# Hybrid block on one core: output projection with 512 moving tokens, its norm spread over later tiles, retention products in place, second buffer for B

## Chip, cores and metric

One Trainium2 chip, one of its cores, one launch. The metric is the device time of that core in microseconds (us); the time before is the median of three runs.

## What is computed

A block for 1024 tokens of 1024 channels, all in float32: a mixer with a retention branch and an S5 branch (a state-space scan) side by side, a projection with residual, attention to a memory of 256 tokens, another projection with residual, and a last norm. Cut to its steps:

```
h = rms_norm(x, norm1_g);  proj = h @ w_in            # 1024 -> q, k, v, g_ret, u, g_s5
ret = retention(rotary(q), rotary(k), v, ret_gn_g) * silu(g_ret)
ssm = s5_branch(u, s5 parameters, glu) * silu(g_s5)
x = x + concat([ret, ssm]) @ w_out
h2 = rms_norm(x, norm2_g);  m = rms_norm(mem, norm_mem_g)
s = einsum(h2 @ wq, m @ wk) * 256 ** -0.5             # 4 heads of 256
o = softmax(s) @ (m @ wv)
x = x + o @ wo
return rms_norm(x, norm_f_g)        # y = x * rsqrt(mean(x * x) + eps) * norm_f_g
```

## The kernel before

**Layout and products.** Activations stand turned: channels on the 128 partitions, tokens along the row. Each large product is made of three matmuls (`mm3`, lines 100 to 103): both operands are split into a high part, rounded to the type float32r, and the low part that is left, and high times high, high times low and low times high are summed in PSUM. `proj_t` (line 105) holds 128x128 weights stationary and moves 512 tokens past them; `proj_nat` (line 511, for `v`) and, before the change, the output projection hold 128 tokens stationary and move 256 weight columns.

**Weights** come in groups of 256 columns. `get_w` (line 88) hands out the group that is loaded and starts the next one; `load_w` (line 70) brings two halves by DMA, ScalarE (ACT) makes the high parts, and VectorE (DVE) or GpSimd (POOL) the low ones. There are two buffers, so one group is in use while the next is made.

**What sets the order.** The program is written in the order of the steps, but a scheduler places each engine's instructions when the kernel is built, by a timeline that it works out from costs of its own, by the dependences, and by when a tile's buffers come free. A tile with one buffer makes the next writer wait for the last reader. `tc.issue_after(x)` is the explicit part: what is written under it is placed only after the instruction `x`.

**The first stage** is a loop of four iterations over pairs of retention heads (from line 612). In each, PE makes `kps` and `qps` (keys and queries), `vps` (values), `gps` (gates), and the retention itself (`knps`, `kvps`, `scps`, `ops`). `retention` leaves a normalised `o`; `ret_store` (line 592) turns it in the next iteration (`rtps`), multiplies it by the gate `silu` into a tile `rt` (three buffers under the tag "st", which the masked scores `st` of line 557 use too) and sends each 512 tokens to the scratch tensor `ret_d` by a DMA on SyncE's queue (SP).

**S5 tables and blocks.** Between these steps `s5_hook` (line 501) prepares the S5 branch: 16 blocks, two to a pair `ct`. `s5_tables(ct)` runs on POOL: it doubles a rotation table `tab` until it has 128 columns (`rotate_double`, lines 320 to 326), sends it to `tab_d`, then makes the pair's factors `B1`, `B2` and `C1` (lines 436 to 454). `s5_prep(b)` (line 457) makes a block's `W` and `VV` on DVE, of which one factor, `t1` (the `t` of the rows, line 476), comes from POOL. `s5_finish(b)` (line 481) transposes `W` on PE (`mps`, line 488) and multiplies `B1` by `VV` (`kps`, line 495). `tab`, `B1`, `B2` and `C1` have one buffer each.

**The end.** `wo_half` (line 1020) makes the output projection for 512 tokens, twice. For each of four weight groups it transposes the residual `xt` on PE (`pxps`, line 1037) and copies it to `on`, then adds the product (`wops`) to it, squares the sum on ACT with a sum along the row, and multiplies by the last norm's weights `gf`, which lie repeated on all partitions. `finish` (line 1059), after the fourth group, takes the reciprocal root of each token's mean square (`rsqrt`, line 119, on DVE), scales the rows and sends 128 tokens in two DMAs to `out`. The first half has the attention of the second half (`attend`) between its groups.

Of the kernel before, what the change touches and what calls it, by code (L numbers as in the profile page):

```python
# [42 lines left out]
CONST_PAD, SSM_PAD, SB_PAD, KA_PAD, QA_PAD, PP_PAD, WO_OFF = 56, 16, 16, 8, 16, 48, 0  # L43
# [3 lines left out]
def block_kernel(ctx: ExitStack, tc: tile.TileContext, a: dict):  # L47
# [100 lines left out]
    d4, i16 = off["d4"], off["i16"]  # L148
# [273 lines left out]
    def s5_tables(ct):  # L422
# [13 lines left out]
        B1 = pr.tile([P, 2 * GB + 1, 16], F32, tag="B1", name=f"B1_{ct}")  # L436
        B2 = pr.tile([P, 2 * GB, 16], F32, tag="B2", name=f"B2_{ct}")
        C1 = pr.tile([P, 2 * GB, 16], F32, tag="C1", name=f"C1_{ct}")
# [15 lines left out]
        g.tensor_scalar(hg(C1), raw[:, :, 2], psgn, None, op0=ALU.mult)  # L454
        per_ct[ct] = raw, B1, B2, C1

    def s5_prep(b):
        gs = slice(b * GB, b * GB + GB)
        ct, hb = b // 2, b % 2
        if hb == 0:  # L460
            s5_tables(ct)
        raw, B1, B2, C1 = per_ct[ct]
        ks = slice(hb * GB, hb * GB + GB)
        raw, B2, C1 = raw[:, hb], B2[:, ks], C1[:, ks]

# [12 lines left out]
        v.tensor_tensor(VV, pw(PR, 9), ve(C1, 9), ALU.mult)
        v.tensor_tensor(t2, pw(PI, 9), ve(raw[:, 3], 9), ALU.mult)
        v.tensor_tensor(VV, VV, t2, ALU.subtract)  # L480
        return W1, VV, B1

# [110 lines left out]
    def ret_store(i, last):  # L593
        o, silu = last
        for h in range(2):
            for n0 in range(0, NCH, 4):
                ps = sm_ps([P, 4, P], "rtps")
                for n in range(4):
                    nc.tensor.transpose(ps[:, n, :], o[:, h, n0 + n, :], ident)
                rt = qp.tile([P, 4, P], F32, tag="st", name=f"rt{i}{h}{n0}", bufs=3)  # L600
                v.scalar_tensor_tensor(rt, ps, gn_g[:, 2 * i + h:2 * i + h + 1],
                                       silu[:, h, n0 * P:n0 * P + 512].rearrange("p (a b) -> p a b", a=4),
                                       op0=ALU.mult, op1=ALU.mult)
                nc.sync.dma_start(out=a["ret_d"][2 * i + h][:, n0 * P:n0 * P + 512],
                                  in_=rt.rearrange("p a b -> p (a b)"))
# [321 lines left out]
    gf = ap_.tile([P, D], F32, name="gf")  # L927
    nc.sync.dma_start(out=gf, in_=a["gf"].to_broadcast([P, D]))
# [91 lines left out]
    def wo_half(half, oT, between):  # L1020
        on = [qap.tile([P, D], F32, tag=("qhi", "qlo")[t % 2], name=f"on{half}{t}") for t in range(4)]
        ssq = [small.tile([P, 5], F32, tag=f"ssq{t}", name=f"ssq{half}{t}") for t in range(4)]
        pre = [z[:, 4:5] for z in ssq]
        for gi in range(4):
            hi, lo = get_w("w_xo", gi)
            xts = []
            for c in range(2):
                xt = pp.tile([P, 512], F32, tag="xt", name=f"xt{half}{gi}{c}", bufs=4)
                nc.sync.dma_start(out=xt, in_=a["x1_d"][2 * gi + c][:, half * 512:half * 512 + 512])
                xts.append(xt)  # L1030
            between(gi)
            cs = slice(gi * 256, gi * 256 + 256)
            for t0 in range(0, 4, 2):
                px = sm_ps([P, 2, 256], "pxps")
                for t in range(2):
                    ts = slice((t0 + t) * P, (t0 + t + 1) * P)
                    for c in range(2):
                        nc.tensor.transpose(px[:, t, c * P:c * P + P], xts[c][:, ts], ident)
                    s.activation(on[t0 + t][:, cs], px[:, t, :], AF.Copy)
                ps = big_ps([P, 2, 512], "wops")  # L1040
                for t in range(2):
                    ts = slice((t0 + t) * P, (t0 + t + 1) * P)
                    for k in range(8):
                        mm3(ps[:, t, 0:256], oT[k][0][:, ts], oT[k][1][:, ts], hi[:, k, :], lo[:, k, :],
                            k == 0, k == 7)
                for t in range(2):
                    x2 = on[t0 + t]
                    v.tensor_tensor(x2[:, cs], ps[:, t, 0:256], x2[:, cs], ALU.add)
                    jk = pp.tile([P, 256], F32, tag="jk", name="jk", bufs=2)
                    s.activation(jk, x2[:, cs], AF.Square, accum_out=ssq[t0 + t][:, gi:gi + 1])  # L1050
                    if gi < 3:
                        v.tensor_tensor(x2[:, cs], x2[:, cs], gf[:, cs], ALU.mult)
                    if gi == 2:
                        v.tensor_reduce(pre[t0 + t], ssq[t0 + t][:, 0:3], axis=AX.X, op=ALU.add)
                        v.tensor_scalar(pre[t0 + t], pre[t0 + t], 1.0 / D, EPS, op0=ALU.mult, op1=ALU.add)
                    if gi == 3:
                        finish(half, t0 + t, x2, ssq[t0 + t][:, 3:4], pre[t0 + t])

    def finish(half, t, x2, last, pre):
        ss = small.tile([P, 1], F32, tag="ssf", name="ssf")  # L1060
        rf = small.tile([P, 1], F32, tag="rf", name="rf")
        v.scalar_tensor_tensor(ss, last, 1.0 / D, pre, op0=ALU.mult, op1=ALU.add)
        rsqrt(rf, ss, 1, "f")
        row = (half * 4 + t) * P
        s.activation(x2[:, 0:512], x2[:, 0:512], AF.Copy, scale=rf)
        nc.sync.dma_start(out=a["out"][row:row + P, 0:512], in_=x2[:, 0:512])
        v.scalar_tensor_tensor(x2[:, 768:D], x2[:, 768:D], rf, gf[:, 768:D], op0=ALU.mult, op1=ALU.mult)
        v.tensor_scalar(x2[:, 512:768], x2[:, 512:768], rf, None, op0=ALU.mult)
        nc.sync.dma_start(out=a["out"][row:row + P, 512:D], in_=x2[:, 512:D])
# [4 lines left out]
    for h in range(4):  # L1074
        attend(0, h, pr0[h], oT0)
        pr1.append(scores(1, h, queries(1, h)))
    wo_half(0, oT0, lambda gi: attend(1, gi, pr1[gi], oT1))
    wo_half(1, oT1, lambda gi: None)
# [12 lines left out]
         ("glu_b", 8), ("invf", 1), ("rsgn", 1), ("nsgn", 1), ("psgn", 1), ("d4", 16), ("i16", 16))  # L1091
# [7 lines left out]
def host_arrays(x, mem, positions, norm1_g, w_in, ret_gn_g, s5_a_re, s5_a_im, s5_log_dt,  # L1099
# [29 lines left out]
    out["gf"] = c(np.asarray(norm_f_g).reshape(1, D))  # L1129
# [63 lines left out]
```

## Time and profile before

| | before |
|---|---|
| median of 3 runs | 1149.53 us (1148.25 to 1150.76) |
| the profiled execution's own time | 1150.77 us |
| its span, first to last instruction | 1148.7 us |
| PE busy | 1118.4 us (97%), 6636 matmuls |
| DVE, ACT, POOL busy | 654.8, 436.6, 241.0 us |
| mean granted TensorE clock | 0.992 of full speed |
| moved by DMA | 171.81 MB, 150 GB/s over the span |

The profile is of one execution, and its span lies inside its own time: 2.1 us are outside. Busy time is the sum of an engine's instructions. A matmul's length in the timeline is longer than the distance to the next one's start, since they are pipelined; the pace is read from start to start. The clock column is the TensorE clock that was granted, as a share of 2.4 GHz.

### The profile page before, as it was taken

Reading aid. Unit: us, or ns where it says so; the run is one execution under the profiler, and the core shown is the slowest. Engines: PE = TensorE matmul, PEld = TensorE weight load, DVE = VectorE, ACT = ScalarE, POOL = GpSimd, SP = SyncE. Lnnn points to the kernel's source line nnn. Section 1 sums busy time; section 2 is a strip of 40 time slices with the busy share of each in tenths; the row PEclk is TensorE's granted clock in tenths of the full one; section 3 lists DMA queues with packets and bytes.
Section 4 is the critical chain, followed back from the end, with each engine's and each line's share of the span. In section 5 each row is a group of like instructions: output and inputs, shape, how many; then the busy total and the mean of one; then the engine's idle time right before and its main releaser. Section 6 shows DMA issues by size and latency. Waiting matters only on the chain.

```text
span 1148.7 us, 17497 instructions
## 1 busy us (share of the span) xinstructions
PE 1118.4 (97%) x6636; PEld 966.3 (84%) x6636; DVE 654.8 (57%) x1388; ACT 436.6 (38%) x863; POOL 241.0 (21%) x342
## 2 busy tenths in 40 slices
PE   8999979999999999999999999999999999999996
PEld 6887957888888888887888888888889888889996
DVE  8896664765663445756585145443645555555564
ACT  7331422432432323434453133233334444344453
POOL 2338798452040001111121100002220000000000
PEclk9999989999999999999999999999999999999999
DMA  6413433442342299898794387443346422122251
GB/s 238 125 38 108 132 127 125 141 157 99 87 139 63 76 244 260 263 275 233 213 294 147 120 228 248 155 156 126 121 152 204 171 72 75 54 74 74 97 198 74
DMA packets 92372, 171.81 MB, mean 150 GB/s; under 512 B 10881, under 2 KB 46977, under 8 KB 92289
## 3 DMA queue, kind: packets, MB, share of 16 engines
q1 hardware_dynamic: 92000, 170.57, 47.2%
q8 instruction: 52, 0.85, 0.3%
q14 instruction: 32, 0.25, 0.1%
q10 hardware_dynamic: 288, 0.14, 0.0%
HBM read 122.04 MB, written 44.43 MB: 145 GB/s over the span
## 4 chain that ended last, share of the span: by engine, by line
PE 80%; POOL 8%; DMA 5%; DVE 4%; issue 1%; ACT 1%; SPq 0%; DVEq 0%; POOLq 0%; ACTq 0%
PE wops L101 3%; PE ups L103 3%; PE wops L103 3%; PE wops L102 3%; PE ups L101 3%; PE qaps L103 3%; PE qaps L102 3%; PE qaps L101 3%; PE obps L102 3%; PE ups L102 3%; PE obps L103 3%; PE glups L103 3%; PE obps L101 3%; PE glups L101 3%; PE glups L102 3%; PE gsps L101 2%
## 5 line engine op out<-in xcount | busy, mean ns | idle before, releaser
L102 PE MATMUL vps<-wlo_w_v,hh 128*128 128x256 f32 x256 | 73.0, 285 | 0.7 <-POOL wlo_w_v L81 0.7
L101 PE MATMUL vps<-whi_w_v,hh 128*128 128x256 f32 x256 | 73.0, 285 | 0.6 <-ACT qs_k L299 0.6
L101 PE MATMUL wops<-whi_w_xo,o 128*128 128x256 f32 x256 | 73.4, 287 | 0.0
L103 PE MATMUL vps<-whi_w_v,hl 128*128 128x256 f32 x256 | 73.0, 285 | 0.0
L103 PE MATMUL wops<-whi_w_xo,o 128*128 128x256 f32 x256 | 71.8, 280 | 0.0
L102 PE MATMUL wops<-wlo_w_xo,o 128*128 128x256 f32 x256 | 71.5, 279 | 0.0
L917 POOL TENSOR_TENSOR sq<-sq,sqx 128x1024 f32<-128x1024 f32 x7 | 19.2, 2738 | 195.3 <-ACT sqx L916 195.3
L101 PE MATMUL gsps<-hh,whi_w_gs 128*128 128x512 f32 x128 | 51.1, 399 | 0.0
L101 PE MATMUL gps<-hh,whi_w_g 128*128 128x512 f32 x128 | 51.0, 399 | 0.0
L101 PE MATMUL ups<-hh,whi_w_u 128*128 128x512 f32 x128 | 50.8, 397 | 0.0
L103 PE MATMUL ups<-hh,wlo_w_u 128*128 128x512 f32 x128 | 50.6, 395 | 0.0
L102 PE MATMUL gps<-hl,whi_w_g 128*128 128x512 f32 x128 | 50.6, 395 | 0.0
L102 PE MATMUL gsps<-hl,whi_w_gs 128*128 128x512 f32 x128 | 50.5, 395 | 0.0
L102 PE MATMUL ups<-hl,whi_w_u 128*128 128x512 f32 x128 | 50.4, 394 | 0.0
L103 PE MATMUL gps<-hh,wlo_w_g 128*128 128x512 f32 x128 | 50.4, 393 | 0.0
L103 PE MATMUL gsps<-hh,wlo_w_gs 128*128 128x512 f32 x128 | 50.3, 393 | 0.0
L101 PE MATMUL oaps<-reth,whi_w_oa 128*128 128x512 f32 x128 | 50.3, 393 | 0.0
L103 PE MATMUL qaps<-h,wlo_w_xq 128*128 128x512 f32 x128 | 50.2, 392 | 0.0
L101 PE MATMUL qaps<-h,whi_w_xq 128*128 128x512 f32 x128 | 50.1, 392 | 0.0
L102 PE MATMUL oaps<-retl,whi_w_oa 128*128 128x512 f32 x128 | 50.0, 391 | 0.0
L102 PE MATMUL qaps<-h,whi_w_xq 128*128 128x512 f32 x128 | 50.0, 390 | 0.0
L102 PE MATMUL obps<-ssmlo,whi_w_ob 128*128 128x512 f32 x128 | 49.9, 390 | 0.0
(394 smaller groups left out, 3372.6 us busy)
## 6 DMA issues: line engine op xcount, KB each, us to landing
CS<-tab_d SPq DMA_DIRECT2D x32, 256.0 KB, 5.9
yr<-y_d SPq DMA_DIRECT2D x16, 512.0 KB, 6.9
wraw_w_xq<-w_xq SPq DMA_DIRECT2D x16, 512.0 KB, 4.1
wraw_w_xo<-w_xo SPq DMA_DIRECT2D x16, 512.0 KB, 4.3
vv_d<-VV SPq DMA_DIRECT2D x16, 288.0 KB, 2.6
VV<-vv_d SPq DMA_DIRECT2D x16, 288.0 KB, 5.1
wraw_w_v<-w_v SPq DMA_DIRECT2D x8, 512.0 KB, 4.3
wraw_w_g<-w_g SPq DMA_DIRECT2D x8, 512.0 KB, 5.1
```

Of the source, the lines that this page charges most:

```text
L101: nc.tensor.matmul(out, wh, xh, start=first, stop=False)
L102: nc.tensor.matmul(out, wh, xl, start=False, stop=False)
L103: nc.tensor.matmul(out, wl, xh, start=False, stop=last)
L917: g.tensor_tensor(sq2, sq2, sq, ALU.add)
```

## The change

1. *Output projection turned* (`wo_half`). Weights are stationary and 512 tokens move, so the result has channels on partitions like the residual, which is added without transposes; `out` is now (8, 128, 1024) and the host turns it. The second half's last two weight groups are done in two parts of 256 tokens.
2. *Its norm.* Squares are ACT's, without sums; POOL (DVE for the fourth group) adds them into `acc`. `token_rms` sums `acc` and the last square over the partitions with matmuls against ones, and takes the reciprocal root; `spread` makes 128 equal rows of it with matmuls; `out` multiplies each tile by its column of `gf` and by these rows and sends it. For all but the last part these steps are placed behind later tiles' additions by `issue_after`. `gf` becomes 8 columns of the packed constants, and two paddings change with it (56 to 48, 0 to 16).
3. *Retention output in place.* `ret_store` writes into `silu`; one DMA of 1024 tokens for two of 512.
4. *B and C.* `B1` has two buffers; `C1` goes, its scaling is done in place in `raw`.

The diff, cut:

```diff
-CONST_PAD, SSM_PAD, SB_PAD, KA_PAD, QA_PAD, PP_PAD, WO_OFF = 56, 16, 16, 8, 16, 48, 0
+CONST_PAD, SSM_PAD, SB_PAD, KA_PAD, QA_PAD, PP_PAD, WO_OFF = 48, 16, 16, 8, 16, 48, 16
...
-        B1 = pr.tile([P, 2 * GB + 1, 16], F32, tag="B1", name=f"B1_{ct}")
+        B1 = pr.tile([P, 2 * GB + 1, 16], F32, tag="B1", name=f"B1_{ct}", bufs=2)
         B2 = pr.tile([P, 2 * GB, 16], F32, tag="B2", name=f"B2_{ct}")
-        C1 = pr.tile([P, 2 * GB, 16], F32, tag="C1", name=f"C1_{ct}")
...
-        g.tensor_scalar(hg(C1), raw[:, :, 2], psgn, None, op0=ALU.mult)
-        per_ct[ct] = raw, B1, B2, C1
+        g.tensor_scalar(raw[:, :, 2], raw[:, :, 2], psgn, None, op0=ALU.mult)
+        per_ct[ct] = raw, B1, B2
...
-        v.tensor_tensor(VV, pw(PR, 9), ve(C1, 9), ALU.mult)
+        v.tensor_tensor(VV, pw(PR, 9), ve(raw[:, 2], 9), ALU.mult)
...
-                rt = qp.tile([P, 4, P], F32, tag="st", name=f"rt{i}{h}{n0}", bufs=3)
-                v.scalar_tensor_tensor(rt, ps, gn_g[:, 2 * i + h:2 * i + h + 1],
-                                       silu[:, h, n0 * P:n0 * P + 512].rearrange("p (a b) -> p a b", a=4),
-                                       op0=ALU.mult, op1=ALU.mult)
-                nc.sync.dma_start(out=a["ret_d"][2 * i + h][:, n0 * P:n0 * P + 512],
-                                  in_=rt.rearrange("p a b -> p (a b)"))
+                rt = silu[:, h, n0 * P:n0 * P + 512].rearrange("p (a b) -> p a b", a=4)
+                v.scalar_tensor_tensor(rt, ps, gn_g[:, 2 * i + h:2 * i + h + 1], rt, op0=ALU.mult, op1=ALU.mult)
+            nc.sync.dma_start(out=a["ret_d"][2 * i + h], in_=silu[:, h, :])
...
-    def wo_half(half, oT, between):
...
+    def wo_half(half, oT, between, steps=()):
+        x2, ws, xts, steps = [], [], [], list(steps)
+        acc = pp.tile([P, 512], F32, tag="acc", name=f"acc{half}", bufs=2)
+        full, ta, tb = slice(0, 512), slice(0, 256), slice(256, 512)
+        for gi, ts in ([(z, full) for z in range(4)] if half == 0 else
+                       [(0, full), (1, full), (2, ta), (3, ta), (2, tb), (3, tb)]):
+            if gi == len(ws):
+                if half and gi < 3:
+                    x2.append(pp.tile([P, 2, 512], F32, name=f"x2_1{gi}"))
+                else:
+                    x2.append(qap.tile([P, 2, 512], F32, tag=("qhi", "qlo")[gi % 2], name=f"x2_{half}{gi}"))
+                ws.append(get_w("w_xo", gi))
+                for c in range(2):
+                    xt = pp.tile([P, 512], F32, tag="xt", name=f"xt{half}{gi}{c}", bufs=4)
+                    nc.sync.dma_start(out=xt, in_=a["x1_d"][2 * gi + c][:, half * 512:half * 512 + 512])
+                    xts.append(xt)
+                between(gi)
+            hi, lo = ws[gi]
+            ps = big_ps([P, 2, 512], "wops")
             for c in range(2):
+                cs = slice(c * P, c * P + P)
+                for k in range(8):
+                    mm3(ps[:, c, ts], hi[:, k, cs], lo[:, k, cs], oT[k][0][:, ts], oT[k][1][:, ts], k == 0, k == 7)
+                xo = x2[gi][:, c, ts]
+                evac = v.tensor_tensor(xo, ps[:, c, ts], xts[2 * gi + c][:, ts], ALU.add)
+                if gi == 0 and c == 0:
+                    s.activation(acc, xo, AF.Square)
+                else:
+                    sq = pp.tile([P, 512], F32, tag="sqo", name=f"sqo{half}{gi}{c}", bufs=2)
+                    s.activation(sq[:, ts], xo, AF.Square)
+                    if gi < 3 or c == 0:
+                        (v if gi == 3 else g).tensor_tensor(acc[:, ts], acc[:, ts], sq[:, ts], ALU.add)
+                for step in steps[:1]:
+                    step(evac)
+                del steps[:1]
+            if gi == 3:
+                steps.extend(finish(half, ts, x2, acc, sq))
+        return steps
+
+    def finish(half, ts, x2, acc, sq):
+        n = (ts.stop - ts.start) // P
+        last = half == 1 and ts.start > 0
+        st = {}
+
+        def token_rms(evac):
+            ps = sm_ps([P, 8], "ms_f")
+            for j in range(n):
+                js = slice(ts.start + j * P, ts.start + j * P + P)
+                nc.tensor.matmul(ps[:, j:j + 1], acc[:, js], ones, start=True, stop=False)
+                nc.tensor.matmul(ps[:, j:j + 1], sq[:, js], ones, start=False, stop=True)
+            msf = small.tile([P, 4], F32, tag="msf", name="msf")
+            rf = small.tile([P, 4], F32, tag="rf", name="rf")
+            v.tensor_scalar(msf[:, :n], ps[:, :n], 1.0 / D, EPS, op0=ALU.mult, op1=ALU.add)
+            rsqrt(rf[:, :n], msf[:, :n], n, "f")
+            st["rf"] = rf
+
+        def spread():
+            rb = sm_ps([P, 512], "rbps")
+            for j in range(n):
+                nc.tensor.matmul(rb[:, j * P:j * P + P], bc(st["rf"][:, j:j + 1], [P, P]), ident, start=True, stop=True)
+            st["rb"] = rb[:, 0:n * P]
+
+        def out(c0, c1):
+            for ct in range(c0, c1):
+                xo = x2[ct // 2][:, ct % 2, ts]
+                v.scalar_tensor_tensor(xo, xo, gfc[:, ct:ct + 1], st["rb"], op0=ALU.mult, op1=ALU.mult)
+                nc.sync.dma_start(out=a["out"][ct][:, half * 512 + ts.start:half * 512 + ts.stop], in_=xo)
+
+        def outs(c0, c1):
+            def step(evac):
+                with tc.issue_after(evac.ins):
+                    out(c0, c1)
+            return step
+
+        def spread_outs(c1):
+            def step(evac):
+                spread()
+                outs(0, c1)(evac)
+            return step
+
+        if half == 0:
+            return [token_rms, spread_outs(2), outs(2, 5), outs(5, 8)]
+        if not last:
+            return [lambda evac: None, token_rms, spread_outs(5), outs(5, 8)]
+
+        def end(evac):
+            token_rms(evac)
+            spread()
+            out(0, 8)
+        return [end]
 
...
-    wo_half(0, oT0, lambda gi: attend(1, gi, pr1[gi], oT1))
-    wo_half(1, oT1, lambda gi: None)
+    last = wo_half(0, oT0, lambda gi: attend(1, gi, pr1[gi], oT1))
+    last = wo_half(1, oT1, lambda gi: None, last)
+    last[0](None)
```

Where it moves instructions, in each engine's order (line, operation, output<-inputs with buffer numbers, shape). First, on POOL, where the second pair's `B1` is written. `tab_2636` is the fifth pair's rotation table, `B_1_1676` the second pair's `B1` and `bcraw_1648` its raw factors; four whole tables stand ahead. Before:

```order
L324 TENSOR_TENSOR tab_2636<-tab_2636 128x4x16
L322 TENSOR_TENSOR tab_2636<-tab_2636,tg_2639 128x4x16
L447 MEMSET B_1_1676 128x16
L448 TENSOR_TENSOR B_1_1676<-bcraw_1648,FR 128x128
L325 TENSOR_TENSOR tg_2639<-tab_2636 128x64
L320 TENSOR_TENSOR tab_2636<-tab_2636 128x4x32
L450 TENSOR_TENSOR B_1_1676<-B_1_1676,tt_1_1679 128x128
```

With the change, `B_1_1669` is that `B1` (`B_0_1340` the first pair's), at the 22nd row of the queue, among the doublings of `rotC` and `rotS` ahead of all tables:

```order
L322 TENSOR_TENSOR rotC<-rotC,tgp 128x32
L447 TENSOR_TENSOR B_0_1340<-bcraw_1312,FR 128x128
L447 TENSOR_TENSOR B_1_1669<-bcraw_1641,FR 128x128
L325 TENSOR_TENSOR tgp<-rotC,rotS 128x32
L320 TENSOR_TENSOR rotC<-rotC 128x32x2
L450 TENSOR_TENSOR B_0_1341<-bcraw_1312,FRs 128x128
```

So the second pair's `B1` moved from the fifth table to the front of the queue, 120 rows up. Second, on POOL, the factor `t` of block 2 (`t_2`), for which `B2` must be there. Before:

```order
L453 TENSOR_TENSOR B_1_1677<-B_1_1677,tt_1_1679 128x128
L322 TENSOR_TENSOR tab_2636<-tab_2636,tg_2639 128x4x32
L476 TENSOR_TENSOR t_2_1689<-PI,B_1_1677 128x512
L449 TENSOR_TENSOR tt_2_1893<-bcraw_1862,FIs 128x128
L325 TENSOR_TENSOR tg_2639<-tab_2636 128x128
```

With the change (`tab_2291` is the fourth pair's table):

```order
L324 TENSOR_TENSOR tab_2291<-tab_2291 128x4x32
L322 TENSOR_TENSOR tab_2291<-tab_2291,tg_2294 128x4x32
L475 TENSOR_TENSOR t_2_1681<-PI,B_1_1670 128x512
L325 TENSOR_TENSOR tg_2294<-tab_2291 128x128
L320 TENSOR_TENSOR tab_2291<-tab_2291 128x4x64
```

It stood in the fifth table, right behind its own pair's `B2`, and is now in the fourth. PE's order changes here too: in the third and fourth iteration `mps` of block 6, and of those at the same place, stands 22 `vps` matmuls behind `kps` of the block before it, where there were 60. Third, on DVE, the end (`on_10040` and `on_10041` are the last two tiles of 128 tokens; `x_10` to `x_13` the second half's four output tiles, `rbps` the rows that `spread` makes). Before:

```order
L1048 TENSOR_TENSOR on_10040<-wops,on_10040 128x256
L1048 TENSOR_TENSOR on_10041<-wops,on_10041 128x256
L1062 SCALAR_TENSOR_TENSOR ssf<-ssq_10044 128x1
L121 TENSOR_SCALAR i_f<-ssf 128x1
L1062 SCALAR_TENSOR_TENSOR ssf<-ssq_10045 128x1
```

With the change:

```order
L1038 TENSOR_TENSOR x_13_9899<-wops,xt_9900 128x256
L126 SCALAR_TENSOR_TENSOR rf<-t_f,rf 128x2
L1045 TENSOR_TENSOR acc_9626<-acc_9626,sqo_10064 128x256
L1079 SCALAR_TENSOR_TENSOR x_10_9627<-x_10_9627,cp,rbps 128x256 x2
L1079 SCALAR_TENSOR_TENSOR x_11_9735<-x_11_9735,cp,rbps 128x256 x2
L1079 SCALAR_TENSOR_TENSOR x_12_9823<-x_12_9823,cp,rbps 128x256
L1038 TENSOR_TENSOR x_13_9899<-wops,xt_9902 128x256
L1079 SCALAR_TENSOR_TENSOR x_12_9823<-x_12_9823,cp,rbps 128x256
L1079 SCALAR_TENSOR_TENSOR x_13_9899<-x_13_9899,cp,rbps 128x256 x2
L1066 TENSOR_SCALAR msf<-ms_f 128x2
```

The first of the two additions (line 1038) of the last group's second part stands ahead of five products of the first part's output, the second behind them, and three products more follow it, then the last norm. Before, the two additions stood side by side, and the norm right behind them.

## Rows read from the trace of the kernel before

**Rows 1.** The page: its first line, and busy time (share, instructions) by engine.

```profile
span 1148.7 us, 17497 instructions
...
PE 1118.4 (97%) x6636; PEld 966.3 (84%) x6636; DVE 654.8 (57%) x1388; ACT 436.6 (38%) x863; POOL 241.0 (21%) x342
```

**Rows 2.** Waits of PE: for what, total, times, longest.

```profile
PE mps L488 <- DVE W L477: 8.3, 1, 8.3
PE ops L567 <- DVE st L557: 3.5, 4, 2.4
```

**Rows 3.** Timeline of PE (start, length, line, out<-in, [idle before, releaser]).

```profile
146.69 0.40 PE L101 MATMUL gps<-hh,whi_w_g 128*128 128x512 f32 x1
...
156.69 0.39 PE L103 MATMUL gps<-hh,wlo_w_g 128*128 128x512 f32 x1
165.43 1.09 PE L488 MATMUL mps<-cp,W 128*128 128x128 f32 x4 [8.35 <-DVE W L477]
...
234.58 0.43 PE L495 MATMUL kps<-VV,B 128*32 128x128 f32 x8
```

**Rows 4.** Windows: length, busy of PE, PEld, DVE, ACT, POOL, clock, DMA, GB/s.

```profile
157.00:160.00 3.00, 0.08 (x1) 0.00 (x0) 1.99 (x3) 0.00 (x0) 3.00 (x6) 0.99 0.00 0
160.00:165.00 5.00, 0.00 (x0) 0.00 (x0) 3.53 (x6) 0.00 (x0) 5.00 (x8) 0.50 0.68 213
...
170.00:171.00 1.00, 1.00 (x5) 0.77 (x5) 1.00 (x2) 0.00 (x0) 1.00 (x2) 0.90 0.08 16
```

**Rows 5.** Timeline of POOL, 105 to 216 us.

```profile
109.33 0.24 POOL L426 COPY tab<-rotC 128x64 f32<-128x64 f32 x1 [2.46 <-DMA tab_d<-tab]
...
119.64 0.28 POOL L432 MEMSET z<- 128x224 f32 x1
...
122.34 0.68 POOL L426 COPY tab<-rotC 128x64 f32<-128x64 f32 x1 [2.42 <-DMA tab_d<-tab]
...
137.68 0.29 POOL L432 MEMSET z<- 128x224 f32 x1
...
144.94 0.96 POOL L322 TENSOR_TENSOR tab<-tab,tg 128x128 f32<-128x128 f32 x1
...
156.55 0.40 POOL L448 TENSOR_TENSOR B<-bcraw,FR 128x128 f32<-128x128 f32 x1
...
163.28 1.10 POOL L476 TENSOR_TENSOR t<-PI,B 128x512 f32<-128x512 f32 x1
...
215.58 0.29 POOL L432 MEMSET z<- 128x224 f32 x1
```

**Rows 6.** Timeline of DVE, 140 to 165 us.

```profile
141.68 0.75 DVE L601 SCALAR_TENSOR_TENSOR rt<-rtps,cp,silu 128x512 f32<-128x512 f32 x1 [8.66 <-DMA ret_d<-rt]
...
164.41 0.88 DVE L477 TENSOR_TENSOR W<-W,t 128x512 f32<-128x512 f32 x1 [1.47 <-POOL t L476]
```

**Rows 7.** Windows of one tile alone, `wops`, then `pxps`: PE, PEld, DVE or ACT.

```profile
1110.00:1135.00 25.00, 25.00 (x204) 23.78 (x204) 3.77 (x10) 1.00 0.20 66
...
1110.00:1135.00 25.00, 3.11 (x17) 1.91 (x16) 3.46 (x10) 1.00 0.20 66
```

**Rows 8.** Timeline of PE, first sums over partitions and first broadcasts.

```profile
37.25 1.84 PE L283 MATMUL ms_n<-ones,xr 128*128 128x1 f32 x16
...
44.33 1.95 PE L134 MATMUL bcps<-cp,r 128*128 128x128 f32 x16
```

**Rows 9.** Timeline of DVE and SP at the end; DMA issues of `rt`.

```profile
1139.60 0.76 DVE L1048 TENSOR_TENSOR on<-wops,on 128x256 f32<-128x256 f32 x2 [0.86 <-PE wops L103]
...
1140.66 0.16 DVE L1062 SCALAR_TENSOR_TENSOR ssf<-ssq 128x1 f32<-128x1 f32 x1 [0.30 <-ACT jk L1050]
...
1143.07 0.48 DVE L1067 SCALAR_TENSOR_TENSOR on<-on,rf,gf 128x256 f32<-128x256 f32 x1
...
1145.20 0.41 SPq L1069 DMA_DIRECT2D out<-on  x1
...
ret_d<-rt SPq DMA_DIRECT2D x16, 256.0 KB, 2.3
```

More of the change, by code (lines that the diff above doesn't have):

```diff
@@ L147, in block_kernel @@
     g2, gm, glu_b, invf, rsgn, nsgn, psgn = (off[z] for z in ("g2", "gm", "glu_b", "invf", "rsgn", "nsgn", "psgn"))
-    d4, i16 = off["d4"], off["i16"]
+    d4, i16, gfc = off["d4"], off["i16"], off["gf"]
     g1 = gp1
@@ L461, in s5_prep @@
             s5_tables(ct)
-        raw, B1, B2, C1 = per_ct[ct]
+        raw, B1, B2 = per_ct[ct]
         ks = slice(hb * GB, hb * GB + GB)
-        raw, B2, C1 = raw[:, hb], B2[:, ks], C1[:, ks]
+        raw, B2 = raw[:, hb], B2[:, ks]
         def pw(tab, n):
@@ L926, in block_kernel @@
     valo = ap_.tile([P, 2, D], F32R, name="valo")
-    gf = ap_.tile([P, D], F32, name="gf")
-    nc.sync.dma_start(out=gf, in_=a["gf"].to_broadcast([P, D]))
     qap = ctx.enter_context(tc.tile_pool(name="qap", bufs=2, reuse_waits="tile"))
@@ L1018, in attend @@
             lst.append((hi, lo))
-    def wo_half(half, oT, between):
[L1021 to L1026, printed above, removed]
-            for c in range(2):
[L1028 to L1069, printed above, removed]
+    def wo_half(half, oT, between, steps=()):
[17 more added lines that the diff above has]
+            ps = big_ps([P, 2, 512], "wops")
+            for c in range(2):
+                cs = slice(c * P, c * P + P)
[16 more added lines that the diff above has]
+        return steps
@@ L1090 @@
 CPACK = (("ident", 128), ("cmask", 128), ("gv", 8), ("geps", 8), ("g128", 4), ("gn_g", 8), ("g2", 8), ("gm", 8),
-         ("glu_b", 8), ("invf", 1), ("rsgn", 1), ("nsgn", 1), ("psgn", 1), ("d4", 16), ("i16", 16))
+         ("glu_b", 8), ("invf", 1), ("rsgn", 1), ("nsgn", 1), ("psgn", 1), ("d4", 16), ("i16", 16), ("gf", 8))
 CPW = sum(z for _, z in CPACK)
@@ L1128, in host_arrays @@
     out["gn_g"] = col(np.asarray(ret_gn_g)[0])
-    out["gf"] = c(np.asarray(norm_f_g).reshape(1, D))
+    out["gf"] = col(norm_f_g)
     out["glu_b"] = col(np.asarray(s5_glu_b)[0][chp])
@@ L1183 @@
            for n, z in arrays.items()}
-    aps["out"] = nc.dram_tensor("out", (L, D), F32, kind="ExternalOutput").ap()
+    aps["out"] = nc.dram_tensor("out", (8, P, L), F32, kind="ExternalOutput").ap()
     with tile.TileContext(nc, schedule_with_timeline_sim=True) as tc:
@@ L1190 @@
     out = np.empty((L, D), np.float32)
-    out[tok_perm()] = np.asarray(r.results[0]["out"])
+    out[tok_perm()] = np.asarray(r.results[0]["out"]).reshape(D, L).T
     return out.reshape(1, L, D)
```

## Prediction

> **What bounds the kernel now.** I began with the page: TensorE (PE) is busy for 1118.4 of 1148.7 us [rows 1], so time can be won in two ways only: less work for PE, or fewer of the 30 us in which it has none. Next I read the waits of PE, the longest first: the first transpose of an S5 block (`mps`) waits 8.3 us for VectorE's `W`, and the retention output (`ops`) waits 3.5 us in four pieces [rows 2]. The timeline shows where the long one lies: the last `gps` matmul starts at 156.69 and nothing follows until 165.43 [rows 3]. The windows show that the wait costs more than itself. The granted clock is 0.99 up to 160, 0.50 from there, and back at full in the slice from 170 [rows 4]: PE had been idle for some 3 us when it fell to the 1.2 GHz level, and 4.7 us of work after 165.43 ran at that level.
>
> Then I followed the wait back. `W` of block 2 is added at 164.41, because GpSimd (POOL) makes its factor `t` only at 163.28 [rows 5, 6]; the wait that the row at 164.41 carries is for POOL. POOL reaches it so late because `B1` has one buffer: the memset that opens the second pair's `B1` stands behind four whole rotation tables in POOL's queue (the first excerpt of the order above). Before that VectorE (DVE) had stood for 8.66 us itself, until the DMA of an earlier `rt` had landed [rows 6]. The end is a chain: the last projection tile is added from 1139.60 on, the norm and four output DMAs follow, and the span ends 9.1 us later [rows 9, 1].
>
> **The change, part by part.** The sum is made against the profiled execution, 1150.77 us, 1.24 above the median of 1149.53.
>
> *Two buffers for B, C in place.* POOL now writes the second pair's B1 and B2 right after the first's, and `t` of block 2 stands in the fourth table, behind the 128-wide `tab` product that began at 144.94 and took 0.96 [rows 5]. Ahead of it POOL gets five products more (two for B1, three for B2 and its scratch), each like the one of 0.40 at 156.55, so 2.2 us with the longer ones among them; of the scalings, one for a pair as before, one moves to the start, where POOL waits anyway. So `t` runs from about 148.1 to 149.2 (1.10, as the row at 163.28), and `W` is whole by 150.2, 6.9 us before PE asks for it at 157.1. The wait of 8.35 goes, and with it the half clock: 4.7 us at half speed did 2.35 us of work. **−10.7 us.** What is late next on that path is `W` of block 3: its `t` stands 21 rows further on, in the fifth table, and by the same shift ends at about 162.4, against PE at 169.0 (48 matmuls of 0.2273 after block 2; 146.69 to 156.69 is 44 of them [rows 3]). The wait of `ops` near 196, 1.0 of the 3.5 us in [rows 2], followed from DVE standing for POOL's `t` of block 4, which now comes 10 us before its use: **−1.0 us**. The earlier 2.4 us near 99 stays, for its cause, DVE's backlog after the S5 parameters, is untouched.
>
> *Retention output in place.* `rt` and its three buffers go, so DVE's 8.66 us go; alone they are worth nothing, since PE has `vps` matmuls until 145.0. SP's queue issues 8 DMAs in place of 16. The new hazard, that `silu` is overwritten before its DMA has read it, is covered: the DMA is issued at about 140, behind the third table's, and `silu` is written at 157. **0.**
>
> *The projection turned.* Of the 768 matmuls of 256 columns, 576 become 288 of 512; 192 stay. One of 256 takes 25.00 us over 204 of them and 17 transposes [rows 7]; taking a transpose, with the change of kind around it, at 0.11, that is 0.1135 to 0.1166, as the transposes' overlap is counted; I take 0.1166, since missing records push it the other way. So 768 × 0.1166 + 64 × 0.11 = 96.6 before, and 288 × 0.2273 + 192 × 0.1166 = 87.9 after: turning itself is worth almost nothing, the 64 transposes of the residual are the gain. To it come 12 sums over partitions in the stream at 0.21 (8 of them, 16 passes, take 1.84 at 37.25, the last one's latency in it) and 6 broadcasts at 0.21 (two passes each; 16 passes take 1.95 at 44.33, again with a latency [rows 8]), 3.8 us. I add 0.8 for one wait that the trace of before doesn't have: the fourth weight group of the second half is used 2.8 us after its buffer comes free, and on DVE three output products stand ahead of its low part. Its bounds: 0, if DVE is ahead, and 3 us, if ScalarE is behind too. **−4.1 us** (96.6 − 87.9 − 3.8 − 0.8). The products with gf, their broadcast load and 32 squares with accumulators leave ScalarE and DVE; they lay beside PE's work and count 0.
>
> *The end.* On DVE five products of the half-finished quarter stand ahead of the last addition (third excerpt). The broadcast they need is 6 matmuls from the end, 0.7 us; five at 0.41 (between the 0.38 of an addition at 1139.60, two in 0.76, and the 0.48 of the product at 1143.07) delay the addition by 1.5. Then 0.84 for addition and square (1.06 from 1139.60 to 1140.66, less the hand-overs counted below), 0.9 sums over partitions, 2.4 reciprocal root (1140.66 to 1143.07), 0.7 broadcast, 8 × 0.41 = 3.3 products, and 3.5 from the last issue to the end (1145.20 to 1148.7) [rows 9, 1]; with 0.2 of hand-overs 13.3 in place of 9.1. **+4.2 us**; with DMAs that land in 2.3, as those of `rt` do [rows 9], +3.0; with the sums and broadcasts at half clock, +5.5.
>
> Sum: −10.7 − 1.0 − 4.1 + 4.2 = −11.6, so 1139.2 on the profiled execution's scale and 1137.9 on the median's. I forecast **1138.5 us**.
>
> **A rule against it.** In the third table POOL needed 15.3 us from 122.34 to 137.68 for the same 21 instructions that took 10.3 from 109.33 to 119.64 [rows 5]; DVE was then in a row of products with both inputs in SBUF. The Trainium skill (SBUF — State Buffer, SBUF: two separate sides) says that DVE and GpSimd share one pair of ports under an exclusive lock, which a DVE instruction with two SBUF inputs takes too; the trace agrees, with those 5.0 us. By the row alone, with DVE's products the same ones as before, the tables keep their pace and the sum stands; by the rule, with DVE's pause gone, each could lose those 5.0 us, and the sum is the first rival's.
>
> **The rivals.** *POOL falls behind, and PE waits at block 6 instead; slower.* PE now meets `mps` of block 6 only 22 `vps` matmuls after `kps` of block 5 (60 before), at 234.58 − 11.7 + 3.0 (0.43 for `kps`, 22 × 0.1166) = 225.9 [rows 3]; `t` for it stands right behind the last table, which ended at 215.9 [rows 5] and by my sum ends at 218.1, so `t` at 219.2 and `W` at about 223.3. If all five tables from the fourth on ran at the third's pace, 5.0 us more each, `t` would end at 244, PE would wait 19 us and lose the 2.35 of the clock: 1160. It decides against the change once POOL is 17 us late. For it: DVE loses its pause of 8.66, in which POOL had the ports. Against: DVE's products are the same ones, only earlier, and POOL was free for 19 us after its tables. 8 in 100.
>
> *The wait moves.* If block 2 or 3 still finds its `W` late by as much as before, 10.7 come back: 1149. For it, POOL is busy without a gap from 157 to 165 [rows 4]; against, a margin of 6.9 and 6.6 us. 7 in 100.
>
> *The projection waits at its weight hand-overs.* POOL, idle in this stretch before, now adds squares, 12 products that DVE's low parts can meet. One of 1.1 us at each of six hand-overs: +6.6, so 1145. Against: most low parts are needed 1 to 2 us after they are done. 13 in 100.
>
> *The S5 stage.* Its loads of tables change places, and two blocks' matmuls move by 8; it holds 3 us of waits that could go or double. It lies inside the range.
>
> **How the numbers follow.** The forecast has 72 in 100. Its own range takes the short end (−1.2), no hand-over wait (−0.8) and 1.5 from the S5 stage on the low side, and 1.3, 2.2 and 1.5 on the high side: 1135 to 1143.5. With the hand-over rival, and an end that is longer by the 1.3 and 0.7 more beside it, the range reaches from **1134.5 to 1147**, leaving out the two rivals of 15 in 100 and some edge. A difference within 0.2% (2.3 us) counts as none: faster 0.85 (forecast and hand-overs), the same 0.07 (the wait moves), slower 0.08 (POOL).
>
> **What would show it.** Right: no wait of `mps` for `W` near 157, no half clock before the end, DVE without a wait for `ret_d`; the stretch from the first `wops` to the last some 4 us shorter; the end 13 us after PE's last projection matmul. Wrong: a half clock anywhere between 150 and 240, POOL's last table later than 225, gaps between `wops`, or an end of 9 us again.

## The result, and the profile after

The changed kernel takes **1158.45 us** (median of 4 runs, 1157.78 to 1162.62) beside 1148.95 us for the kernel before (4 runs): ratio 1.0086, 95% interval 1.0058 to 1.0114. It is 0.9% slower, where 1.0% faster was forecast (1138.5 beside 1149.53), and outside the range of 1134.5 to 1147. The profiled execution took 1157.78 us.

The page of the changed kernel, its first line and busy times [rows 1]:

```profile
span 1156.0 us, 16722 instructions
...
PE 1119.5 (97%) x6332; PEld 955.0 (83%) x6332; DVE 656.0 (57%) x1287; ACT 415.0 (36%) x779; POOL 260.5 (23%) x354
```

PE is as busy as before with 304 matmuls fewer, so the time is in waits and in half clock (a granted clock of 0.50). The waits of PE [rows 2], as what for, total, times, longest:

```profile
PE mps L487 <- DVE silu L600: 12.8, 1, 12.8
PE ops L566 <- DVE st L556: 3.0, 2, 2.8
PE rbps L1073 <- DVE rf L126: 2.5, 1, 2.5
PE ms_f L1063 <- ACT sqo L1043: 2.2, 1, 2.2
...
PE wops L103 <- DVE wlo_w_xo L81: 1.1, 3, 0.7
```

The wait of 8.3 us for `W` is gone, and one of 12.8 stands in its place, for another instruction. The windows show the first gone and the second there [rows 4] (busy time of PE, PEld, DVE, ACT, POOL, clock, DMA share, GB/s):

```profile
157.00:160.00 3.00, 3.00 (x23) 2.20 (x22) 2.84 (x5) 0.60 (x1) 0.55 (x3) 1.00 0.62 219
160.00:165.00 5.00, 5.00 (x24) 4.14 (x23) 0.00 (x0) 0.00 (x0) 5.00 (x15) 1.00 0.94 274
...
225.00:235.00 10.00, 0.00 (x0) 0.00 (x0) 2.16 (x2) 0.00 (x0) 0.00 (x0) 0.67 0.78 222
235.00:240.00 5.00, 4.08 (x24) 3.48 (x24) 4.89 (x8) 0.60 (x1) 0.00 (x0) 0.50 0.29 118
```

To see where the time went, I read in the timeline of PE when each stage's first matmul starts (us from the span's start):

| first of | before | after | later by |
|---|---|---|---|
| `gps`, first iteration | 60.08 | 59.81 | -0.3 |
| `rtps`, second iteration | 125.88 | 126.10 | +0.2 |
| `ups`, so the first stage's end | 356.70 | 362.57 | +5.9 |
| `glups`, so the S5 stage's end | 681.06 | 684.66 | +3.6 |
| `wops` | 1026.31 | 1029.23 | +2.9 |
| last `wops` | 1139.29 | 1142.04 | +2.8 |
| end of the span | 1148.7 | 1156.0 | +7.3 |

The first stage lost 5.9 us where 11.7 were to be won; the projection gave 0.2 where 4.1 were forecast; the end costs 4.5, as forecast (4.2). The S5 stage gave 2.3 and the stretch from `glups` to `wops` 0.7, but nothing shows that the change did it: the profile of before has a wait of 1.95 near 527 for a low part of the weights, with half clock behind it, which r_only and w_only below, with the S5 stage of before, don't have either (321.5 and 321.8 us from the first `ups` to the first `glups`; 324.4 before, 322.1 after).

**The new wait, followed back.** PE, then DVE, in the timeline [rows 3, 6]:

```profile
222.82 0.27 PE L598 MATMUL rtps<-cp,o 128*128 128x128 f32 x1
235.92 1.12 PE L487 MATMUL mps<-cp,W 128*128 128x128 f32 x4 [12.82 <-DVE silu L600]
```

```profile
214.14 1.21 DVE L309 TENSOR_TENSOR rot_k<-qs_k,cosT 128x1024 f32<-128x1024 f32 x1
215.28 1.48 DVE L310 TENSOR_TENSOR sw_k<-sw_k,sinT 128x1024 f32<-128x1024 f32 x1
216.68 1.42 DVE L309 TENSOR_TENSOR rot_q<-qs_q,cosT 128x1024 f32<-128x1024 f32 x1
232.84 1.23 DVE L310 TENSOR_TENSOR sw_q<-sw_q,sinT 128x1024 f32<-128x1024 f32 x1 [14.73 <-DMA sw_q<-qs_q]
...
235.12 0.75 DVE L600 SCALAR_TENSOR_TENSOR silu<-rtps,cp,silu 128x512 f32<-128x512 f32 x1
```

This is `mps` of block 5, and it doesn't wait for its `W`, which was whole at 206.2. It needs a PSUM buffer, which the gate product of line 600 frees; that product stands in DVE's queue behind the rotation of `q`, and the rotation waits for 14.73 us for `sw_q`, the copy of `q` with its halves exchanged, which goes by DMA. ACT had finished its source at 211.23. In SP's queue:

```profile
222.49 0.33 SPq L430 DMA_DIRECT2D tab_d<-tab  x1
222.91 0.39 SPq L433 DMA_DIRECT2D k_d<-z  x1
...
225.75 2.42 SPq L303 DMA_DIRECT2D sw_q<-qs_q  x4
```

`tab_d` is the store of the eighth rotation table, and SP takes its queue in order: `sw_q` stood behind a table that nothing needs before the S5 stage. Before the change the order was the same, but PE came later. There the store went out at 215.55, `qs_q` was whole only at 221.10, `sw_q` went at 221.12, and DVE waited for it for 0.43 us. SP's queue, then DVE, before:

```profile
215.55 0.33 SPq L430 DMA_DIRECT2D tab_d<-tab  x1
...
220.53 0.33 SPq L76 DMA_DIRECT2D wraw_w_kq<-w_kq  x1
221.12 2.62 SPq L303 DMA_DIRECT2D sw_q<-qs_q  x4
```

```profile
227.17 1.23 DVE L310 TENSOR_TENSOR sw_q<-sw_q,sinT 128x1024 f32<-128x1024 f32 x1 [0.43 <-DMA sw_q<-qs_q]
```

So the 11.7 us of PE's gain had little slack to go into. Five smaller issues stand between the store and `sw_q`; after the change they took 3.3 us with the store (222.49 to 225.75). At that pace `sw_q` could have gone out at about 218.8 before the change, 2.3 us sooner than it did (an estimate from these rows). And the table itself came 6.9 us later than before, 222.49 instead of 215.55. So `sw_q` went out 4.6 us later than before, not sooner, and DVE's product with it started 5.7 us later. Why the table was late: three of its instructions on POOL after the change, and the same three before [rows 5]:

```profile
214.15 1.53 POOL L322 TENSOR_TENSOR tab<-tab,tg 128x128 f32<-128x128 f32 x1
215.75 1.27 POOL L325 TENSOR_TENSOR tg<-tab 128x128 f32<-128x128 f32 x1
216.99 1.59 POOL L320 TENSOR_TENSOR tab<-tab 128x256 f32<-128x256 f32 x1
```

```profile
209.41 0.45 POOL L322 TENSOR_TENSOR tab<-tab,tg 128x128 f32<-128x128 f32 x1
209.94 0.40 POOL L325 TENSOR_TENSOR tg<-tab 128x128 f32<-128x128 f32 x1
210.30 0.61 POOL L320 TENSOR_TENSOR tab<-tab 128x256 f32<-128x256 f32 x1
```

They take 4.39 in place of 1.46 us while DVE makes its three rotation products from 214.14 to 218.10, two inputs in SBUF each; before the change these products ran from 223.26 on, after the table. That is 2.9 of the 6.9 us; 2.4 came with the table's start (208.52, before 206.16), and 1.7 is a wait for the landing of the seventh table's `z` (zeros for `k_d`), whose DMA stood behind `sw_k`.

### The profile page after: what moved, and what is told of

Same layout as the page of the kernel before. It is cut to its first block, busy times and chain, and to the rows that moved or that the text cites. A ratio compares the mean times of both kernels' runs of the same rounds, so it can differ in the third digit from the quotient of the medians.

```text
span 1156.0 us, 16722 instructions
## 1 busy us (share of the span) xinstructions
PE 1119.5 (97%) x6332; PEld 955.0 (83%) x6332; DVE 656.0 (57%) x1287; ACT 415.0 (36%) x779; POOL 260.5 (23%) x354
## 4 chain that ended last, share of the span: by engine, by line
PE 76%; POOL 9%; DMA 7%; DVE 5%; issue 2%; SPq 1%; ACT 1%; DVEq 0%; ACTq 0%; POOLq 0%
PE ups L103 3%; PE ups L101 3%; PE qaps L103 3%; PE qaps L101 3%; PE qaps L102 3%; PE obps L102 3%; PE ups L102 3%; PE obps L103 3%; PE glups L101 3%; PE obps L101 3%; PE glups L103 3%; PE glups L102 3%; PE gsps L102 2%; PE gsps L101 2%; PE gsps L103 2%; PE wops L101 2%
## 5 line engine op out<-in xcount | busy, mean ns | idle before, releaser
L1045 POOL TENSOR_TENSOR acc<-acc,sqo 128x512 f32<-128x512 f32 (+1 forms) x12 | 15.8, 1320 | 253.6 <-issue 187.3
L103 PE MATMUL wops<-o,wlo_w_xo 128*128 128x512 f32 (+1 forms) x160 | 56.0, 351 | 1.1 <-DVE wlo_w_xo L81 1.1
L101 PE MATMUL wops<-o,whi_w_xo 128*128 128x512 f32 (+1 forms) x160 | 56.1, 351 | 0.5 <-DVE x L1038 0.5
L102 PE MATMUL wops<-o,whi_w_xo 128*128 128x512 f32 (+1 forms) x160 | 55.7, 348 | 0.0
L102 PEld LDWEIGHTS vps<-wlo_w_v,hh 128*128 128x128 f32 x256 | 49.2, 192 | 0.9 <-issue 0.6
```

Source lines behind the costliest of these rows:

```text
L101: nc.tensor.matmul(out, wh, xh, start=first, stop=False)
L102: nc.tensor.matmul(out, wh, xl, start=False, stop=False)
L103: nc.tensor.matmul(out, wl, xh, start=False, stop=last)
L1045: (v if gi == 3 else g).tensor_tensor(acc[:, ts], acc[:, ts], sq[:, ts], ALU.add)
```

## The experiments

Each kernel of a group ran beside the kernel before on the same chip; ratios are to that one, with 95% intervals.

### One part at a time

*b_only* has only the hunks of `B1` and `C1`, *r_only* only those of `ret_store`, *w_only* only those of `wo_half`, `finish`, `gf` and the paddings.

```diff
-        B1 = pr.tile([P, 2 * GB + 1, 16], F32, tag="B1", name=f"B1_{ct}")
+        B1 = pr.tile([P, 2 * GB + 1, 16], F32, tag="B1", name=f"B1_{ct}", bufs=2)
...
```

> Only the second buffer for B1 and the scaling of C in place, on the kernel before. Theory one (queue): PE comes 11.7 us earlier to the transposes of the third iteration and stands there, since VectorE waits for the swapped copy of q (sw_q), whose DMAs stand in SP's queue behind the store of the last rotation table, which GpSimd finishes no earlier than before. Then this part alone carries the loss of the first stage: the first ups matmul some 5 us later than the 356.7 of before, a wait of PE of 10 us or more near 225 to 236, 1154 us. Theory two (gate in place): the wait comes from the retention products written into silu, whose instruction the trace names as the releaser; then this part alone gives the forecast gain, the first ups matmul near 345, 1138 us.

Measured: 1154.66 us, ratio **1.0063** (1.0044 to 1.0081). In its profiled execution (1160.54 us) the first `ups` starts at 363.70, and PE waits:

```profile
238.40 1.11 PE L487 MATMUL mps<-cp,W 128*128 128x128 f32 x4 [11.28 <-DVE rt L600]
```

The releaser is the gate product again, here the old one into `rt`. This part alone carries the first stage's loss, and the theory of the gate in place falls.

> Only the retention products in place, on the kernel before. Theory one: GpSimd's and SP's order around the last table stays, PE still waits near 165 for W of block 2: no difference beyond 1.5 us, 1149 us. Theory two: the in-place products bring the new wait of PE of some 12 us near 225, 1160 us.

Measured: 1147.23 us, ratio 0.9994 (0.9974 to 1.0014), no difference. Its trace holds a lesson. In that execution PE was 2.0 us late from the start (first `gps` at 62.08), then the clock was at 0.50 from about 101 to 111, so that the first `rtps` came 6.0 us late (131.92, before 125.88). The stage still ended at 356.80: in the timeline of PE the wait at block 2 is 6.3 us shorter:

```profile
165.15 0.63 PE L488 MATMUL mps<-cp,W 128*128 128x128 f32 x4 [2.02 <-DVE W L477]
```

Six us taken from PE cost nothing there: POOL's chain to `W` of block 2 sets when PE goes on, and PE's wait is what is left over.

> Only the turned projection and its norm, on the kernel before. Theory one: the first stage is as before (first ups at 356.7), the stretch from the first to the last wops is within 0.5 us of the 113.0 of before, the end from the last wops is 4.5 us longer: 1153 us. If the sum of the prediction holds for this part by itself (stretch 4.1 shorter, end 4.2 longer): 1149 us.

Measured: 1153.41 us, ratio **1.0043** (1.0022 to 1.0064). From the first to the last `wops` 112.82 us (1026.01 to 1138.83; before 112.98), from there to the end 13.7 (before 9.4). The turned projection wins nothing and pays the end in full.

### The swapped copies from another queue

```diff
-                nc.sync.dma_start(out=sw[32 * b:32 * b + 32, :], in_=qs[o:o + 32, :])
+                nc.scalar.dma_start(out=sw[32 * b:32 * b + 32, :], in_=qs[o:o + 32, :])
```

> The changed kernel, with the swapped copies for the rotation issued from ScalarE's queue, right behind the copy that they read, and not from SP's. Theory one (queue): sw_q lands near 216, VectorE does not stop, PE waits at most 3 us near 223 for W of the next block, no half clock: 12.8 and 2.5 us less, 1145 us. Theory two (gate in place) and a theory three, that GpSimd's last table itself holds everything: PE still waits 10 us or more near 225, 1157 us.

Measured: 1158.57 us, ratio 1.0078 (1.0046 to 1.0111): no gain, so the theory as I had it is wrong. On ACT's queue the issue itself stood:

```profile
215.94 1.00 ACT L299 ACTIVATE qs_q<-qps 128x1024 f32<-128x1024 f32 x1
216.97 10.46 ACTq L303 DMA_DIRECT2D sw_q<-qs_q  x3
227.48 2.03 ACT L589 ACTIVATE o<-o,nb,rs 128x128 f32<-128x128 f32 x5 [10.53 <-DMA k_d<-z]
```

Three issues took 10.46 us, and what released them was the landing of `k_d<-z`, the eighth table's other store, of another queue. The built program says why: each DMA waits for the earlier DMA that has the same one of eight completion counters (DMAHW0 to 7), and the counters are handed out in turn over both queues, SP's and ACT's, in the scheduled order. The two stores in SP's queue and the copies in ACT's, with the waits of each:

```
L430 DMA tab_d<-tab_3597 128x1024 [waits DMAHW6_49,Pool_49]
L433 DMA k_d<-z_3620 128x2x112 [waits DMAHW7_49,Pool_49]

L303 DMA sw_q_2240<-qs_q_2238 32x1024 [waits DMAHW4_49,Activation_49]
L303 DMA sw_q_2240<-qs_q_2238 32x1024 [waits DMAHW6_49]
L303 DMA sw_q_2240<-qs_q_2238 32x1024 [waits DMAHW7_49]
L303 DMA sw_q_2240<-qs_q_2238 32x1024 [waits DMAHW0_49]
```

So it is the place in the order that counts here, not the queue. PE's wait changed its place with it: `o`, which `rtps` turns, now stood on ACT behind that issue.

```profile
228.02 0.47 PE L598 MATMUL rtps<-cp,o 128*128 128x128 f32 x1 [5.28 <-ACT o L589]
```

It is shorter than 12.82, but PE also came later in this execution (first `rtps` of the second iteration at 133.91, in the change 126.10), and the first `ups` started at 363.87, no sooner than in the change.

### The eighth table's stores behind the copies

```diff
+        def store(out, in_):
+            if ct == 7:
+                with tc.issue_after(sw_last["q2"].ins):
+                    nc.sync.dma_start(out=out, in_=in_)
+            else:
+                nc.sync.dma_start(out=out, in_=in_)
-        nc.sync.dma_start(out=a["tab_d"][ct], in_=tab)
+        store(a["tab_d"][ct], tab)
...
```

and the same for the store of `z`; `sw_last["q2"]` is the third iteration's last `sw_q` DMA. *late_store* is the changed kernel with it, *before_late_store* the kernel before, *br_late_store* the changed kernel with the old projection.

> The changed kernel, with the eighth table's two stores (tab_d and k_d) put behind the third iteration's copies sw_q in SP's queue, by issue_after. Theory one, now sharper (all DMAs share eight completion counters that are handed out in the order of the program, so that sw_q behind those stores waits for GpSimd's last table from any queue): sw_q is issued near 212, VectorE goes on at 218, the wait of 12.8 us and the 2.5 us of half clock go, at most 3 us of other waits come: 1143 to 1146 us. Theory three (GpSimd's last table itself, through t and W, holds PE): no gain beyond 3 us, 1155 us or more.

> The same order on the kernel before, with its one buffer for B1. Theory one: the wait of 8.3 us for W of block 2 stays, PE then reaches the rotation of the third iteration when sw_q has landed anyway (VectorE waited 0.43 us for it before): no difference beyond 2 us, 1146 to 1149 us.

> The second buffer, C and the gate in place, the order of late_store, and the projection of before. Theory one: the gain of late_store, and without the 4.3 us that the turned projection adds at the end: 1138 to 1141 us, so 7 to 9 us faster than the kernel before. If the projection's part were of use in company: slower than late_store.

| | stores as scheduled | stores late |
|---|---|---|
| kernel before | 1 | 1.0014 (0.9999 to 1.0030) |
| the change | 1.0086 (1.0058 to 1.0114) | **0.9966** (0.9952 to 0.9980), 1144.23 us |
| the change, old projection | not run | **0.9933** (0.9912 to 0.9954), 1140.34 us |

The order alone is worth nothing, the second buffer alone loses (b_only), the two together win: theory one. These runs move the place in SP's queue and the counter together; that the counters alone can hold a copy rests on swap_act. Theory three, that the table itself holds PE, falls: in late_store the table was later still, its store going out at 227.48, and yet the wait at the place of the 12.82 us is gone, and `W` comes last, barely:

```profile
230.37 0.63 PE L494 MATMUL mps<-cp,W 128*128 128x128 f32 x4 [0.17 <-DVE W L483]
```

### Is the gate in place of use?

*b_late_store* is the kernel before with the hunks of `B1` and `C1` and the late stores.

> The kernel before with the second buffer for B1, C in place and the late stores of the eighth table; gate and projection as before. Theory one: all of the gain of the first stage comes from these two together, the gate in place adds nothing: as br_late_store, 1139 to 1142 us. If the gate in place is needed for it (VectorE stood for ret_d before): 1144 us or more.

Measured: 1145.47 us, ratio 0.9966 (0.9950 to 0.9982), beside 0.9933 (0.9912 to 0.9954) with the gate in place. DVE and PE in b_late_store (profiled execution: 1148.66 us):

```profile
231.62 0.75 DVE L607 SCALAR_TENSOR_TENSOR rt<-rtps,cp,silu 128x512 f32<-128x512 f32 x1 [3.88 <-DMA ret_d<-rt]
```

```profile
233.91 0.63 PE L494 MATMUL mps<-cp,W 128*128 128x128 f32 x4 [3.40 <-DVE W L483]
```

The fourth `rt` needs one of three buffers, and the store that frees it now stands behind the eighth table's. In place there is no such wait. So this part, worth nothing alone, is worth about 4 us in company (0.33% between the ratios); the two intervals touch, and the ratios by themselves would not show it, but PE's wait of 3.40 us does.

### Squares on VectorE

```diff
-                        (v if gi == 3 else g).tensor_tensor(acc[:, ts], acc[:, ts], sq[:, ts], ALU.add)
+                        v.tensor_tensor(acc[:, ts], acc[:, ts], sq[:, ts], ALU.add)
```

> late_store with all sums of squares of the projection on VectorE, none on GpSimd. If GpSimd's additions stretch VectorE's low parts of w_xo at the last weight group (4.12 us for four, beside 2.49 for the four ahead), those four fall to some 2.5 us and PE's three waits for them, 1.15 us in all, go. If it is VectorE's own queue (products with the norm ahead of the low parts), the four stay within 2.5 us but the waits stay at 1 us or more, since VectorE has more to do.

Measured once, 1144.37 us; what counts is the trace. POOL's additions and the four low parts of the last weight group in late_store, then the low parts in acc_vector:

```profile
1107.30 2.92 POOL L1052 TENSOR_TENSOR acc<-acc,sqo 128x512 f32<-128x512 f32 x2 [6.95 <-ACT sqo L1050]
```

```profile
1107.26 4.12 DVE L81 TENSOR_TENSOR wlo_w_xo<-wraw_w_xo,whi_w_xo 128x512 fp32r<-128x512 f32 x4
```

```profile
1107.87 2.49 DVE L81 TENSOR_TENSOR wlo_w_xo<-wraw_w_xo,whi_w_xo 128x512 fp32r<-128x512 f32 x4
```

PE's waits for them fall from 1.15 to 0.25 us, and the stretch from the first to the last `wops` from 112.8 to 111.5. So POOL's additions had stretched DVE's low parts; it was not DVE's own queue. The time from the last `wops` to the end did not fall (14.8 us, in late_store 14.4).

### Further along the same chain

*st_first* is br_late_store with the products of S5 blocks 0 to 2 (lines 475 to 480) under an `issue_after` of the first iteration's second `st`; *st_first_table_last* has, besides, `s5_tables(7)` under one of the `t` of block 6; *stores_in_turn* has, besides, this:

```diff
-            if ct == 7:
-                with tc.issue_after(sw_last["q2"].ins):
+            if ct in (3, 4, 7):
+                with tc.issue_after((k_store[ct - 1] if ct < 7 else sw_last["q2"]).ins):
...
```

Here `k_store[b]` is the DMA that stores `K` of block `b`.

> br_late_store with VectorE's products of S5 blocks 0 to 2 put behind the first masked scores (st) of the first iteration. The wait of PE of 3.05 us near 99, and the half clock that follows it in some runs, go. If GpSimd's last table now holds PE (W of block 6 came last by 0.2 us in late_store), most of it comes back as a wait for that W near 225: 1139 to 1141 us. If not: 1134 to 1137 us.

> The same, and the eighth table's work on GpSimd put behind the factor t of block 6. If GpSimd's last table holds PE in st_first, that wait goes too and the gain is kept: 1134 to 1137 us. If it doesn't: as st_first.

> st_first_table_last, with the stores of the fourth and fifth tables put behind the store of K of the block that PE does meanwhile (blocks 2 and 3), as the eighth's behind sw_q. In st_first_table_last ScalarE stood 13.2 us near 170 for the landing of k_d from K, whose store stood behind the fourth table's in SP's queue, and PE 4.4 us. If every wait that is left in the first stage is of this one kind, it goes here too: 1135 to 1138 us. If GpSimd's tables, now later, hold PE through t and W: 1139 to 1142 us.

Measured: 1140.54 (0.9935, 0.9909 to 0.9961), 1140.94 (0.9926, 0.9903 to 0.9949) and **1136.59 us** (0.9883, 0.9855 to 0.9911, 6 runs). In the first the wait of 3.05 us near 99 went, and one came at block 3, at 170.98:

```profile
170.98 0.63 PE L500 MATMUL mps<-cp,W 128*128 128x128 f32 x4 [3.97 <-ACT whi_w_v L80]
```

I had looked for it near 225, by the last table; there none came, and so st_first_table_last could win nothing. In st_first_table_last, where the same wait is 4.40 us long, ACT shows what it was:

```profile
170.15 0.28 ACT L514 ACTIVATE K<-kps 128x128 f32<-128x128 f32 x1 [13.19 <-DMA k_d<-K]
```

ACT stood 13.19 us for the landing of the small `K` store, which was issued behind the fourth table's. It is the same kind of wait. In stores_in_turn PE has no wait near 170, and ACT's is 7.07 us: the fastest version here, 1.2% below the kernel before, though its interval overlaps those of the two versions ahead of it. One such wait is left in it, 4.3 us of DVE for `sw_q` until 218.27, and PE stands 4.3 us for it at 222.

## Why the prediction was wrong, point by point

- **What bounded the kernel before**: right. `t` of block 2 ran at 148.38 (forecast 148.1), and the 8.35 us, the half clock behind them and the 1.0 us near 196 went. The step that failed is the next one, "What is late next on that path": I followed POOL's `t` and DVE's `W` alone, and so took the -10.7 and -1.0 as won for the whole stage. PE came to block 5's transposes at 223.1 and stood there for 12.82, with another 2.9 of half clock (from 235.9 to about 242, the prediction's own sign of being wrong) and 1.6 in shorter new waits near 170 and 180: 17.3 of the 17.6 us between -11.7 and +5.9. I had counted SP's queue by its number of DMAs, not by what stands in it: the store of a table ahead of a copy that DVE needs.
- **The first rival** came near the place (block 5, not 6) and the time (1160, at 8 in 100), but that was luck, for it had another mechanism: the last table was 7 us late, not 25, and `t` of block 6 was done at 223.87, long before PE went on. By its own condition, 17 us, it would not have decided. What decided is that `sw_q` had some 2.3 us of slack, less than the table was late.
- **The second rival** (`W` of block 2 or 3 late by as much as before) did not come, but the margin of 6.6 us given for block 3 was gone: its `W` was whole at 169.5, 0.3 after PE came, and PE waited 0.47. DVE stood 8.79 us there for ACT's `K`, and ACT for a store of the same kind as in st_first_table_last:

```profile
168.38 0.28 ACT L497 ACTIVATE K<-kps 128x128 f32<-128x128 f32 x1 [10.00 <-DMA k_d<-K]
```

- **Retention in place, 0**: right alone (0.9994), wrong in company, about 4 us.
- **The projection, -4.1**: mis-sized; measured -0.2, in the change and in w_only. From start to start in the timeline, before: the 256-column matmuls 0.119 and the transposes 0.070, 96.0 us in all. That this is near the 96.6 of the forecast is luck: the transposes had been put at 0.11, the matmuls at 0.1166. After: 288 at 0.231 and 192 at 0.126, hand-overs in it, so 90.8 (forecast 87.9), with waits of 1.65 (forecast 0.8) and sums and broadcasts of 3.5 (forecast 3.8). The pace of the 192 is the largest piece. Of the waits, 1.1 came from POOL's squares, the third rival's mechanism, at one hand-over of the six; acc_vector shows them fall to 0.25.
- **The end, +4.2**: right, 4.5; from the last `wops` to the end 14.0 us (forecast 13.3 from PE's last matmul).
- **The S5 stage** gave 2.3 us, more than the 1.5 allowed for it; runs without the change have the shorter stage too, so it is no gain of the change.
- **The rule against the change**: the Trainium skill (SBUF — State Buffer, SBUF: two separate sides) says that of DVE and GpSimd the one that comes second to the shared ports is blocked. The trace agrees in that both engines lose: 2.9 us of the eighth table and 0.9 of PE's waits in the projection. It was not 5.0 for each table: the instructions of the fourth to the seventh, added up from the timeline, stayed within 1.3 us of before. But those of the eighth took 12.2 us (before 9.5) with DVE standing beside them, and 14.9 in late_store, where DVE goes on. So some 5 us were right for that one table, and late_store is faster all the same, since `sw_q` no longer stands behind its store.

In sum: -11.7 became +5.9, -4.1 became -0.2, and +4.2 became +4.5; with the -2.3 and -0.7 of the stretches between, which are not the change's as far as the runs show, that is the +7.3 of the span.

## What to carry to other kernels

A wait that is removed is worth only the slack of the next chain that ends at the same place; here PE's wait was what was left over beside a chain of POOL, SP and DVE, and a delay of PE of 6 us cost nothing either. Before a gain is counted, read on each in-order queue (the DMA queue too, and the counters that its transfers share) what stands ahead of the first thing that is needed earlier, and when that is done. A bulk store that nothing needs soon belongs behind the small copy that an engine waits for.

## What the hardware showed that I had not expected

- DVE and POOL slow each other: POOL's table instructions took 1.27 to 1.59 us in place of 0.40 to 0.61 beside DVE's rotation products, and DVE's low parts 1.03 in place of 0.62 each beside POOL's additions. Apart they have their old times (0.41 for POOL's 128x128 product at 183.61 in the same kernel, 0.62 for DVE's low parts in acc_vector).
- After a wait of PE of 2.4 to 2.8 us near 100 the granted clock fell to its half level in some executions and not in others. After 2.36 us it stayed at 1.00 in the profile of before and fell to 0.50 in r_only; after 2.82 it stayed at 1.00 in the change's profile, and in b_only, after 2.80, the windows show:

```profile
100.00:105.00 5.00, 3.47 (x15) 3.05 (x16) 2.46 (x6) 0.00 (x0) 4.13 (x13) 0.65 0.53 135
105.00:110.00 5.00, 5.00 (x32) 4.10 (x31) 1.23 (x9) 1.08 (x2) 4.69 (x9) 0.50 0.00 0
110.00:115.00 5.00, 5.00 (x19) 4.05 (x20) 2.18 (x10) 0.00 (x0) 2.47 (x10) 0.83 0.36 131
```

About 5 us of PE's work are lost in it (10 us at 0.50), which may be one source of the spread of single runs; in r_only PE's wait for `W` of block 2 was that much shorter, and it cost nothing. Why it falls in one execution and not in another was not tried.
